# Hybrid decoder layer on one core: four raw weight tiles, the up products in another order, the gate as one function

## The chip, the cores and the metric

One Trainium2 chip, one core. The metric is the device time of one execution in microseconds (us); the kernel before takes 2186.93 us, the median of 3 runs (2183.86 to 2192.37).

## The reference

A decoder layer over 1024 positions of width 1024, in fp32: a gated feed-forward part (FFN) with half weight, a token-mixing part (RWKV-7 beside a chunked gMLP, from one input projection into one output projection), a second FFN, and a last norm.

```python
def swiglu(h, w1, w3, w2):
    return (jax.nn.silu(h @ w1) * (h @ w3)) @ w2

for l in range(DEPTH):            # DEPTH = 1, D_MODEL = 1024, D_FF = 2816
    x = x + FFN_RES_SCALE * swiglu(rmsnorm(x, ffn1_norm[l]), ffn1_w1[l], ffn1_w3[l], ffn1_w2[l])
    h = rmsnorm(x, mix_norm[l])
    p = h @ w_in[l]
    y_rwkv = rwkv7_mixer(p[..., :D_SHIFT], ...)
    y_gmlp = gmlp_mixer(p[..., D_SHIFT:D_SHIFT + GMLP_WIDTH], p[..., D_SHIFT + GMLP_WIDTH:], ...)
    x = x + jnp.concatenate([y_rwkv, y_gmlp], axis=-1) @ w_out[l]
    x = x + FFN_RES_SCALE * swiglu(rmsnorm(x, ffn2_norm[l]), ffn2_w1[l], ffn2_w3[l], ffn2_w2[l])
return rmsnorm(x, final_norm)
```

## The kernel before

**Numbers and products.** Every large fp32 product is made of three fp32r matmuls: each operand is held as a high part (ACT copies it into the fp32r tile) and a low part (DVE or POOL subtract the high part from the source), and the three of the four pairs in `HI_LO` are accumulated in PSUM. The positions are two halves ("rows") of 512, the features likewise. Each FFN matrix product is done with seven products of half-sized operands instead of eight, by sums and differences of the quarters; the products are numbered 1 to 7.

**Stages of an FFN.**
- `first_half` does product 1 of both up matrices with row 0: 22 steps (w1 and w3 by turns, 11 column blocks), 24 matmuls each. Its result goes to DRAM (`sd`) for the other products; its gated value goes to `hd[1]`.
- Meanwhile a background task, `build`, makes the operands of products 3 to 7 (`x_build`: per round of four, four tiles `nx` are loaded, all four normed on DVE (L297), added and subtracted, and split into `xc`). When it is done, its pool is closed, a new pool `pw` is opened and the first weights `wraw` are loaded into it.
- `up` does products 6, 5, 7, 4, 3 in 22 steps of 60 matmuls (L192 issues all of them, `prod` takes 12 per product). `up_prep` makes the five weight operands of the step ahead on DVE (L386 to L392) and splits them into `wup`, a ring of eight. Five PSUM evacuations on DVE (L447, L451, L453, L458, L462) add the products to `s1`; product 7 is accumulated in the bank of product 6 and product 3 in that of product 5. On even steps (w1) the gate is a tanh on ACT (L327) and one DVE operation (L328), on odd steps (w3) a DVE product (L330). Every second step `out` makes `hd[2]` to `hd[7]` on POOL and stores them.
- `down` does products 1, 5, 2, 3, 6, 7, 4, each in 11 steps of 12 matmuls. A step's `operands` loads a weight tile and a tile of `hd` into one `raw` tile (ring of two; L479, L480 issue the loads on SP's queue), combines the weight with `tst` on DVE (L483 in product 5, L485 in 7, L487 in 4, L495 in 3), copies both halves on ACT (L490, L491) and subtracts on DVE (L492, weight) and POOL (L493, h) into a `wsp` tile (ring of four). After a product DVE adds its banks to the residual tiles `rd` or `res` (L527); a finished residual is squared (L230 on ACT, L232 on DVE).

A norm's sum of squares goes over the partitions by `spread`: 8 small matmuls, a power on POOL (L220), and 4 matmuls that spread it back (L201).

**The mixer** stands between the FFNs: `w_in`, `lora_up`, gMLP, the RWKV chain as background work, `w_out`. Its weight tiles come through the same ring `raw` of two (`wtile`, `w_out`). `lora_up` makes three results per block in an `xs` tile (ring of two) and a `silu` tile (ring of three), and stores each to DRAM (L875). `first_half` of FFN2 starts with row 0; at its step 12 at the latest a hook puts in `w_out` of row 1, then the remaining steps follow, with `build` beside them.

**What sets the order.** The program is written as generators. `Flow` steps them by a clock of its own (the numbers behind `yield`), the tile framework then orders each engine's instructions by priority (`evac()` puts the evacuations of PSUM ahead) and by its own timing of them, and each engine works through its list in that order. Weight loads and most stores share SP's queue. A tile of a ring comes free, and its next load may be issued, only when its last reader is done.

## Time and profile before

| | |
|---|---|
| median of 3 runs | 2186.93 us (2183.86 to 2192.37) |
| profiled execution, its own time | 2188.83 us |
| its span in the trace | 2187.0 us |
| mean granted clock of TensorE | 0.956 |
| busy: PE, weight loads | 1999.5 us (91%), 1617.7 us (74%) |
| busy: DVE, ACT, POOL | 1272.0 us (58%), 702.2 us (32%), 987.7 us (45%) |
| HBM read, written | 260.53 MB, 93.34 MB |
| stages: first_half of FFN1, its up, its down | 25.9 to 160.5, to 472.4, to 738.2 us |
| mixer with w_out and FFN2's first_half, up's start | to 1593.65 us |
| up of FFN2, its down, last spread and output | to 1903.8, to 2166.0, to 2187.0 us |

PE is TensorE's matmuls, PEld its weight loads. Busy time counts an instruction from its start to its end; idle time before an instruction is put down to what released it last. The granted clock is the share of TensorE's full speed that the throttle gave; matmul durations in the records overlap, so the price of one is best taken from a run of many.

### The profile page before, as it was taken

Reading aid. Unit: us, or ns where it says so; the run is one execution under the profiler, and the core shown is the slowest. Engines: PE = TensorE matmul, PEld = TensorE weight load, DVE = VectorE, ACT = ScalarE, POOL = GpSimd, SP = SyncE. Lnnn points to the kernel's source line nnn. Section 1 sums busy time; section 2 is a strip of 40 time slices with the busy share of each in tenths; the row PEclk is TensorE's granted clock in tenths of the full one; section 3 lists DMA queues with packets and bytes.
Section 4 is the critical chain, followed back from the end, with each engine's and each line's share of the span. In section 5 each row is a group of like instructions: output and inputs, shape, how many; then the busy total and the mean of one; then the engine's idle time right before and its main releaser. Section 6 shows DMA issues by size and latency. Waiting matters only on the chain.

```text
span 2187.0 us, 34516 instructions
## 1 busy us (share of the span) xinstructions
PE 1999.5 (91%) x13408; PEld 1617.7 (74%) x13408; DVE 1272.0 (58%) x1749; ACT 702.2 (32%) x1202; POOL 987.7 (45%) x749
## 2 busy tenths in 40 slices
PE   6999999997998998999999989989789999979986
PEld 5777777786776677777888778867577777858764
DVE  7828777745457464454543354324877777544565
ACT  5442222213444443252212232224422222224432
POOL 4426666643444664353322232223566666434432
PEclk9999999998998999998999997999989999989988
DMA  6754444435544577453534463336644444375443
GB/s 217 239 170 160 151 160 164 165 141 209 187 135 150 180 258 218 114 202 106 172 101 118 121 191 109 119 112 211 223 148 148 148 158 164 110 251 181 133 153 116
DMA packets 232884, 356.15 MB, mean 163 GB/s; under 512 B 67984, under 2 KB 100752, under 8 KB 232720
## 3 DMA queue, kind: packets, MB, share of 16 engines
q1 hardware_dynamic: 178944, 338.23, 46.5%
q10 hardware_dynamic: 53776, 15.71, 3.1%
q8 instruction: 105, 1.72, 0.3%
q14 instruction: 59, 0.48, 0.1%
HBM read 260.53 MB, written 93.34 MB: 162 GB/s over the span
## 4 chain that ended last, share of the span: by engine, by line
PE 22%; DMA 11%; DVE 8%; issue 5%; POOL 3%; ACT 1%; SPq 0%; POOLq 0%; ACTq 0%; DVEq 0%
PE psd L192 12%; PE pse L192 4%; PE pse L201 3%; DMA raw<-in_ffn_w_dram 3%; DMA raw<-hd 2%; PE psc L201 2%; DMA wraw<-in_ffn_w_dram 1%; POOL wsp L493 1%; DMA raw<-in_w_out_dram 1%; POOL wsp L712 1%; DVE wsp L492 1%; DVE rd L527 1%; POOL wup L257 1%; DMA tdr<-D 1%; DMA M<-ldr 1%
## 5 line engine op out<-in xcount | busy, mean ns | idle before, releaser
L192 PE MATMUL psd<-xt,wsp 128*128 128x512 f32 x1920 | 484.7, 408 | 19.4 <-ACT silu L353 9.0
L192 PEld LDWEIGHTS psd<-xt,wsp 128*128 128x128 f32 x1920 | 363.6, 193 | 115.7 <-ACT silu L353 12.1
L192 PE MATMUL psd<-xc,wup 128*128 128x512 f32 x1584 | 376.0, 394 | 37.2 <-DVE z L447 20.3
L192 PEld LDWEIGHTS psd<-xc,wup 128*128 128x128 f32 x1584 | 298.0, 189 | 108.7 <-DVE z L447 23.8
L712 POOL TENSOR_TENSOR wsp<-raw,wsp 128x512 fp32r<-128x512 f32 x170 | 234.3, 1398 | 317.7 <-ACT wsp L709 317.5
L192 PE MATMUL psd<-wsp 128*128 128x512 f32 x1440 | 351.0, 402 | 27.4 <-ACT wsp L491 14.9
L192 PEld LDWEIGHTS psd<-wsp 128*128 128x128 f32 x1440 | 274.0, 193 | 97.5 <-ACT wsp L491 16.7
L493 POOL TENSOR_TENSOR wsp<-raw,wsp 128x512 fp32r<-128x512 f32 x154 | 210.3, 1368 | 293.7 <-ACT wsp L491 241.3
L257 POOL TENSOR_TENSOR wup<-wraw,wup 128x512 fp32r<-128x512 f32 x132 | 200.6, 1528 | 117.7 <-ACT wup L256 112.4
L192 PE MATMUL pse<-xc,wup 128*128 128x512 f32 x1056 | 248.0, 390 | 0.0
L192 PEld LDWEIGHTS pse<-xc,wup 128*128 128x128 f32 x1056 | 198.4, 188 | 41.4 <-ACT wup L256 0.2
L709 ACT CAST wsp<-raw 128x512 fp32r<-128x512 f32 x246 | 140.5, 618 | 152.5 <-PE psd L192 58.2
L492 DVE TENSOR_TENSOR wsp<-raw,wsp 128x512 fp32r<-128x512 f32 x110 | 96.2, 876 | 104.8 <-ACT wsp L490 104.3
L256 ACT CAST wup<-wraw 128x512 fp32r<-128x512 f32 x132 | 81.1, 619 | 223.5 <-PE pse L192 151.8
L192 PE MATMUL pse<-wsp 128*128 128x512 f32 x396 | 118.3, 416 | 31.2 <-DVE wsp L492 18.1
L491 ACT CAST wsp<-raw 128x512 fp32r<-128x512 f32 x154 | 95.4, 620 | 124.2 <-DMA raw<-hd 114.2
L490 ACT CAST wsp<-raw 128x512 fp32r<-128x512 f32 x110 | 68.0, 618 | 195.2 <-DMA raw<-in_ffn_w_dram 107.8
L192 PEld LDWEIGHTS pse<-wsp 128*128 128x128 f32 x396 | 75.2, 197 | 59.3 <-DVE wsp L492 22.0
L192 PE MATMUL psc<-wsp 128*128 128x512 f32 x396 | 111.6, 408 | 0.0
L257 POOL TENSOR_TENSOR wup<-wt,wup 128x512 fp32r<-128x512 f32 x44 | 63.4, 1440 | 69.7 <-ACT wup L256 58.7
L256 ACT CAST wup<-wt 128x512 fp32r<-128x512 f32 x88 | 53.6, 617 | 120.3 <-PE psd L192 100.9
L192 PEld LDWEIGHTS psc<-wsp 128*128 128x128 f32 x396 | 78.4, 199 | 17.5
(216 smaller groups left out, 2620.6 us busy)
## 6 DMA issues: line engine op xcount, KB each, us to landing
wraw<-in_ffn_w_dram SPq DMA_DIRECT2D x88, 512.0 KB, 4.5
raw<-hd SPq DMA_DIRECT2D x154, 256.0 KB, 3.3
raw<-in_ffn_w_dram SPq DMA_DIRECT2D x132, 256.0 KB, 3.1
raw<-in_ffn_w_dram SPq DMA_DIRECT2D x44, 512.0 KB, 4.0
raw<-in_w_in_dram SPq DMA_DIRECT2D x36, 512.0 KB, 3.6
hd<-u SPq DMA_DIRECT2D x66, 256.0 KB, 2.0
hd<-s SPq DMA_DIRECT2D x66, 256.0 KB, 2.1
sd<-silu SPq DMA_DIRECT2D x44, 256.0 KB, 3.2
```

Source lines behind the costliest of these rows:

```text
L192: i = self.nc.tensor.matmul(*args, **kw)
L201: i = self.nc.tensor.matmul(*args, **kw)
L256: nc.scalar.copy(t[:, 0], src)
L257: eng.tensor_tensor(t[:, 1], src, t[:, 0].bitcast(F32), op=ALU.subtract)
L490: nc.scalar.copy(t[:, 0, 0], w)
L491: nc.scalar.copy(t[:, 0, 1], h)
L492: ve.tensor_tensor(t[:, 1, 0], w, t[:, 0, 0].bitcast(F32), op=ALU.subtract)
L493: ge.tensor_tensor(t[:, 1, 1], h, t[:, 0, 1].bitcast(F32), op=ALU.subtract)
L527: ve.scalar_tensor_tensor(rv, sets[y][f], 0.25, rv, op0=ALU.mult, op1=ALU.add)
L709: self.nc.scalar.copy(dst[:, 0, sl], src[:, sl])
L712: eng.tensor_tensor(dst[:, 1, sl], src[:, sl], dst[:, 0, sl].bitcast(F32), op=ALU.subtract)
```

## The change

It has five parts.
- The ring `raw` has four tiles (`RAWB`) instead of two, in `wtile`, `down` and `w_out`; `wsp` keeps four. To make room, squares are put elsewhere (in row 1 of FFN1's down into a `raw` tile), `lora_up` puts its three results into three `silu` tiles, and in `up` the ring `z` has 3 tiles for 6, `s` 4 for 5, with `s1` in a ring of its own of 3.
- `up` does products 6, then 4 of the step before, 5, 7, 3. Products 6 and 7 have banks of their own (`d`), as 5 and 3 have (`e`); product 4 is accumulated on its step's product 7. There are still five evacuations per step. `up_prep` splits product 3's weight ahead of product 4's.
- The gate on even steps is ACT's Silu alone; the factor in `down` goes from 0.25 to 0.5, since the tanh form gave twice the value.
- `apply` stores row 0's normed tiles to DRAM (`xn`), and `x_build` loads them instead of norming row 0 again.
- In FFN2, `pw` is opened and the first weights are loaded ahead of `x_build`, and row 1's spread stands right behind `w_out`.

```diff
+RAWB = 4
...
-    def squares(self, pool, acc, t):
+    def squares(self, pool, acc, t, name="xs", bufs=2):
...
-            s = pool.tile([P, 2, HALF], F32, name="xs", bufs=2)
+            s = pool.tile([P, 2, HALF], F32, name=name, bufs=bufs)
...
-    def apply(self, dst, res, gain, rb):
+    def apply(self, dst, res, gain, rb, out=None):
...
+            if out is not None:
+                nc.sync.dma_start(out[k], t)
...
-            nc.sync.dma_start(t, src[row][k // 2][:, k % 2])
+            nc.sync.dma_start(t, src[row][k // 2][:, k % 2] if row else self.xn[k])
...
-            for k, t in zip(ks, ts):
-                normed(*k, t)
+            for k, t in zip(ks[:2], ts):
+                ve.scalar_tensor_tensor(t, t, self.v(gain, k[1]), rb[0], op0=ALU.mult, op1=ALU.mult)
...
-                nc.scalar.activation(u, c, AF.Tanh, scale=0.5)
-                nc.vector.scalar_tensor_tensor(u, u, 1.0, c, op0=ALU.add, op1=ALU.mult)
+                nc.scalar.activation(u, c, AF.Silu)
...
+        ws[3] = sp(b22, ge)
         ws[4] = sp(b21, ge)
-        ws[3] = sp(b22, ge)
...
-        def z(name="z", bufs=6):
+        def z(name="z", bufs=3):
...
-                s1s[s] = z()
+                s1s[s] = z("s1", 3)
...
-            b, c = self.psum("d"), self.psum("e")
-            s1 = s1s.pop(s)
-            yield from prod(s, 6, b, True, False)
-            with self.evac():
-                w12 = z()
-                ve.tensor_add(w12, b, s1)
-            yield from prod(s, 5, c, True, False)
-            yield from prod(s, 7, b, False, True)
-            with self.evac():
-                ve.tensor_add(s1, b, s1)
-                w22 = z()
-                ve.tensor_add(w22, c, s1)
-            self.gate(us, u, s, 22, w22)
-            d = self.psum("d")
-            yield from prod(s, 4, d, True, True)
-            with self.evac():
-                ve.tensor_add(s1, d, s1)
-            self.gate(us, u, s, 21, s1)
-            yield from prod(s, 3, c, False, True)
-            with self.evac():
-                ve.tensor_add(w12, c, w12)
-            self.gate(us, u, s, 12, w12)
+        def tail(s, b, w12):
+            yield from prod(s, 4, b, False, True)
+            with self.evac():
+                ve.tensor_add(w12, b, w12)
+            self.gate(us, u, s, 21, w12)
...
+            s1 = s1s.pop(s)
+            a = self.psum("d")
+            yield from prod(s, 6, a, True, True)
+            with self.evac():
+                w12 = s1
+                ve.tensor_add(w12, a, s1)
+            if last is not None:
+                yield from tail(*last)
+            c = self.psum("e")
+            yield from prod(s, 5, c, True, True)
+            with self.evac():
+                v = z()
+                ve.tensor_add(v, c, w12)
+            b = self.psum("d")
+            yield from prod(s, 7, b, True, False)
+            with self.evac():
+                w22 = z()
+                ve.tensor_add(w22, b, v)
+            self.gate(us, u, s, 22, w22)
+            d = self.psum("e")
+            yield from prod(s, 3, d, True, True)
+            with self.evac():
+                ve.tensor_add(v, d, v)
+            self.gate(us, u, s, 12, v)
+            last = (s, b, w12)
+        yield from tail(*last)
...
-            raw = self.ws.tile([P, 2, HALF], F32, name="raw", bufs=2)
+            raw = self.ws.tile([P, 2, HALF], F32, name="raw", bufs=RAWB)
...
-                        ve.scalar_tensor_tensor(rv, sets[y][f], 0.25, rv, op0=ALU.mult, op1=ALU.add)
+                        ve.scalar_tensor_tensor(rv, sets[y][f], 0.5, rv, op0=ALU.mult, op1=ALU.add)
...
-    def build(self, src, gain, w, rb, stats, ready):
+    def build(self, src, gain, w, rb, stats, ready, early=False):
...
+        if early:
+            self.pw, self.cpw = self.open("pw")
         pool, cb = self.open("pb")
         yield from stats(pool)
+        if early:
+            self.raw0 = self.up_load(self.pw, w, 0)
         yield from self.x_build(pool, self.xc, src, gain, rb)
...
-                self.squares(self.xq, accs[row], res[row][kp])
+                self.squares(*((self.ws, accs[1], res[1][kp], "raw", RAWB) if row else (pool, accs[0], res[0][kp])))
...
-            yield from self.w_out(1, xres, accs[1])
+            p1, c1 = self.open("p1")
+            yield from self.w_out(1, xres, accs[1], (p1,))
 
             def stats2(pool):
-                cxq.close()
-                rb = yield from self.spread(accs[1], "e")
-                rbs2.append(self.keep(rb, pool))
-
-            flow.spawn(self.build(xres[1], "g2", w2, rbs2, stats2, ("xb", 1)))
+                yield 0.1
+                rbs2.append(self.keep(rb1, pool))
+
+            rb1 = yield from self.spread(accs[1], "e")
+            c1.close()
+            cxq.close()
+            flow.spawn(self.build(xres[1], "g2", w2, rbs2, stats2, ("xb", 1), True))
...
-                    t = self.xq.tile([P, 2, HALF], F32, name="xs", bufs=2)
-                    ts = [t[:, 0], t[:, 1], self.xtp.tile([P, HALF], F32, name="silu", bufs=3)]
+                    ts = [self.xtp.tile([P, HALF], F32, name="silu", bufs=3) for _ in range(3)]
```

Three places in the order of the instructions. On PE, from w_out of row 1 (`psd<-wsp`) over the rest of first_half (`psd<-xt,wsp`) to the first up product (`psd<-xc,wup`), `one,xs` and `con,rr_r` being the spread, before:

```order
L192 MATMUL psd<-wsp 128x512 x192
L192 MATMUL psd<-xt,wsp 128x512 x33
L201 MATMUL pse<-one,xs 128x1 x8
L192 MATMUL psd<-xt,wsp 128x512 x9
L201 MATMUL pse<-con,rr_r 128x128 x4
L192 MATMUL psd<-xt,wsp 128x512 x174
L192 MATMUL psd<-xc,wup 128x512 x2
```

and now:

```order
L193 MATMUL psd<-wsp 128x512 x192
L202 MATMUL pse<-one,xs 128x1 x8
L202 MATMUL pse<-con,rr_r 128x128 x4
L193 MATMUL psd<-xt,wsp 128x512 x216
L193 MATMUL psd<-xc,wup 128x512 x2
```

The spread's two groups stood among the matmuls of first_half and now stand ahead of them.

On DVE, at the end of product 1 of FFN2's down (`wsp<-raw` are its last splits, `dt` the weights kept for the later products, combined for product 5, and `rd<-psd` the evacuations of product 1), before:

```order
L492 TENSOR_TENSOR wsp<-raw,wsp 128x512 x7
L483 TENSOR_TENSOR dt<-raw,dt 128x512
L492 TENSOR_TENSOR wsp<-dt,wsp 128x512
L527 SCALAR_TENSOR_TENSOR rd<-psd,rd 128x512 x3
L483 TENSOR_TENSOR dt<-raw,dt 128x512
L527 SCALAR_TENSOR_TENSOR rd<-psd,rd 128x512 x9
L483 TENSOR_TENSOR dt<-raw,dt 128x512
L492 TENSOR_TENSOR wsp<-dt,wsp 128x512
L483 TENSOR_TENSOR dt<-raw,dt 128x512
```

and now:

```order
L502 TENSOR_TENSOR wsp<-raw,wsp 128x512 x7
L493 TENSOR_TENSOR dt<-raw,dt 128x512 x2
L502 TENSOR_TENSOR wsp<-dt,wsp 128x512
L493 TENSOR_TENSOR dt<-raw,dt 128x512
L502 TENSOR_TENSOR wsp<-dt,wsp 128x512
L493 TENSOR_TENSOR dt<-raw,dt 128x512
L537 SCALAR_TENSOR_TENSOR rd<-psd,rd 128x512 x3
L502 TENSOR_TENSOR wsp<-dt,wsp 128x512
L537 SCALAR_TENSOR_TENSOR rd<-psd,rd 128x512 x9
L493 TENSOR_TENSOR dt<-raw,dt 128x512
```

Three more combinations and one more split of product 5 now stand ahead of the first evacuations.

On SP, at the start of FFN2's down (`dt` the kept weights, `raw` the operands' loads, `hd_10` stores of the last up step), before:

```order
L677 DMA rd<-xres_1_3_98 128x1024
L514 DMA dt<-in_ffn_w_dram 128x512 x6
L479 DMA raw<-in_ffn_w_dram 128x512
L480 DMA raw<-hd_6_153 128x512
L514 DMA dt<-in_ffn_w_dram 128x512
L479 DMA raw<-in_ffn_w_dram 128x512
L480 DMA raw<-hd_7_154 128x512
L514 DMA dt<-in_ffn_w_dram 128x512 x4
```

and now:

```order
L428 DMA hd_10_201<-s 128x512
L696 DMA rd<-xres_1_3_98 128x1024
L430 DMA hd_10_223<-u 128x512
L524 DMA dt<-in_ffn_w_dram 128x512 x2
L432 DMA hd_10_212<-s 128x512
L524 DMA dt<-in_ffn_w_dram 128x512 x2
L435 DMA hd_10_179<-s 128x512
L524 DMA dt<-in_ffn_w_dram 128x512 x4
L489 DMA raw<-in_ffn_w_dram 128x512
L490 DMA raw<-hd_8_155 128x512
```

The stores of the last step now stand among the loads, and where six loads of `dt` stood ahead of the load for step 6 (`hd_6`), eight stand ahead of that for step 8.

## Rows read from the trace of the kernel before

**Rows 1.** Page, part 1: busy us, share of span and instructions of each engine.

```profile
PE 1999.5 (91%) x13408; PEld 1617.7 (74%) x13408; DVE 1272.0 (58%) x1749; ACT 702.2 (32%) x1202; POOL 987.7 (45%) x749
```

**Rows 2.** Chain that ended last, in up of FFN2: start us, us, engine, tile, line, count.

```profile
1871.32 8.16 PE psd L192 x36
```

**Rows 3.** Stretches, L192: window, length, PE busy, PEld busy, granted clock, DMA share, GB/s.

```profile
160.50:474.90 314.40, 302.58 (x1320) 246.70 (x1321) 1.00 0.44 150
...
472.40:738.20 265.80, 233.06 (x937) 180.54 (x936) 0.94 0.54 179
...
1511.30:1593.60 82.30, 57.38 (x220) 43.20 (x220) 0.88 0.66 221
...
1593.60:1911.90 318.30, 309.31 (x1340) 253.25 (x1341) 0.99 0.41 144
...
1903.80:2165.90 262.10, 228.88 (x937) 178.92 (x935) 0.95 0.53 173
...
2048.90:2078.80 29.90, 29.90 (x134) 24.75 (x133) 1.00 0.44 127
...
2078.80:2127.60 48.80, 36.09 (x133) 26.32 (x132) 0.86 0.43 145
```

**Rows 4.** Timeline of PE, start of FFN2's second half: start us, us, instruction [idle before].

```profile
1511.33 9.49 PE L192 MATMUL psd<-xt,wsp 128*128 128x512 f32 x33 [4.80 <-DVE res L760]
...
1584.52 1.22 PE L192 MATMUL psd<-xc,wup 128*128 128x512 f32 x2 [7.60 <-ACT wup L256]
...
1593.65 4.65 PE L192 MATMUL psd<-xc,wup 128*128 128x512 f32 x12 [7.05 <-DVE wup L257]
```

**Rows 5.** Timeline of PE, down of both FFNs.

```profile
506.42 10.95 PE L192 MATMUL psd<-wsp 128*128 128x512 f32 x36 [4.94 <-ACT wsp L491]
...
2092.15 1.65 PE L192 MATMUL pse<-wsp 128*128 128x512 f32 x3 [4.54 <-DVE wsp L492]
```

**Rows 6.** Waits of ACT in down: us in total, times, longest us.

```profile
ACT wsp L491 <- DMA raw<-hd: 114.2, 71, 8.0
...
ACT wsp L490 <- DMA raw<-in_ffn_w_dram: 107.8, 43, 15.9
```

**Rows 7.** Page, part 6, DMA issues: loads of raw, KB each, median us to landing.

```profile
raw<-in_ffn_w_dram SPq DMA_DIRECT2D x132, 256.0 KB, 3.1
```

**Rows 8.** Groups of DVE in down: busy us, mean ns, idle us before and its releasers.

```profile
L492 DVE TENSOR_TENSOR wsp<-raw,wsp 128x512 fp32r<-128x512 f32 x110 | 96.2, 876 | 104.8 <-ACT wsp L490 104.3
...
L232 DVE TENSOR_TENSOR xs<-xs 128x1024 f32<-128x1024 f32 x24 | 32.4, 1350 | 23.6 <-ACT xs L230 23.6
...
L527 DVE SCALAR_TENSOR_TENSOR rd<-psd,rd 128x512 f32<-128x512 f32 x44 | 28.0, 678 | 0.9 <-PE psd L192 0.9
...
L485 DVE TENSOR_TENSOR raw<-dt,raw 128x512 f32<-128x512 f32 x22 | 19.3, 877 | 28.0 <-DMA raw<-in_ffn_w_dram 26.1 <-DMA raw<-hd 1.9
```

**Rows 9.** Waits of PE: for the evacuation of product 6 of up.

```profile
PE psd L192 <- DVE z L447: 20.3, 12, 2.6
```

**Rows 10.** Timeline of PE, last spread of the program.

```profile
2170.75 3.57 PE L201 MATMUL pse<-one,xs 128*128 128x1 f32 x16 [4.71 <-DVE xs L232]
...
2175.66 2.08 PE L201 MATMUL pse<-con,rr_r 128*128 128x128 f32 x8 [1.34 <-POOL rr_r L220]
```

**Rows 11.** Group of DVE in x_build: the normalisation.

```profile
L297 DVE SCALAR_TENSOR_TENSOR nx<-nx,vec,rbk 128x512 f32<-128x512 f32 x32 | 33.1, 1050 | 7.2 <-ACT rbk L280 3.6 <-DMA nx<-xres 3.2 <-DMA nx<-in_x_dram 0.4
```

**Rows 12.** Line L875, lora_up's stores: ns min/median/max on SP, us to landing.

```profile
L875 SPq DMA_DIRECT2D lo<-xs x16: 319/452/1362, 775.4 to 972.4; - x16
...
DMA to landing us min/median/max: 2.0/3.5/6.4
```

**Rows 13.** Groups of the gate and of ACT's table loads.

```profile
L328 DVE SCALAR_TENSOR_TENSOR u<-u,z 128x512 f32<-128x512 f32 x66 | 61.6, 937 | 23.9 <-ACT u L327 23.9
...
L1043 ACT ACT_TABLE_LOAD x2 | 2.6, 1283 | 2.3 <-DVE gmean L1235 2.3
```

**Rows 14.** Line L390, DVE in the preparation of up's weights: ns min/median/max.

```profile
L390 DVE TENSOR_TENSOR wraw<-wraw x44: 677/1750/1784, 90.4 to 1871.0; 128x512 f32<-128x512 f32 x44
```

More of the change, by code (lines that the diff above doesn't have):

```diff
@@ L292, in load @@
             t = new()
-            nc.sync.dma_start(t, src[row][k // 2][:, k % 2])
+            nc.sync.dma_start(t, src[row][k // 2][:, k % 2] if row else self.xn[k])
             return t
-        def normed(row, k, t):
-            ve.scalar_tensor_tensor(t, t, self.v(gain, k), rb[row], op0=ALU.mult, op1=ALU.mult)
         def put(p, kk, t, eng):
@@ L466, in up @@
             ws.pop(s)
+        u = lambda: z("u", 6)
+        prep(0)
+        last = None
+        for s in range(ns):
+            prep(s + 1)
+            s1 = s1s.pop(s)
[24 more added lines that the diff above has]
+        yield from tail(*last)
     def down(self, pool, w2, res, done):
@@ L534, in build @@
                    for p in (6, 5, 7, 4, 3)}
+        if early:
+            self.pw, self.cpw = self.open("pw")
         pool, cb = self.open("pb")
         yield from stats(pool)
+        if early:
+            self.raw0 = self.up_load(self.pw, w, 0)
         yield from self.x_build(pool, self.xc, src, gain, rb)
         cb.close()
-        self.pw, self.cpw = self.open("pw")
-        self.raw0 = self.up_load(self.pw, w, 0)
+        if not early:
+            self.pw, self.cpw = self.open("pw")
+            self.raw0 = self.up_load(self.pw, w, 0)
         self.flow.done.add(ready)
@@ L571, in program @@
         self.hd = {p: [self.dr.tile([P, HALF], F32, name=f"hd{p}_{j}") for j in range(NP)] for p in range(1, 8)}
+        self.xn = [self.dr.tile([P, HALF], F32, name=f"xn{k}") for k in range(KT)]
         self.sd = [self.dr.tile([P, HALF], F32, name=f"sd{j}") for j in range(2 * NP)]
@@ L580, in program @@
         x12 = self.halves()
-        rbs = [self.keep(rb)]
-        self.apply(x12, rx, "g1", rb)
+        rbs = []
+        self.apply(x12, rx, "g1", rb, self.xn)
         cb.close()
@@ L644, in program @@
         accs = ([], [])
-        out0 = yield from self.w_out(0, xres, accs[0])
+        out0 = yield from self.w_out(0, xres, accs[0], (self.mp, "h", 3))
         rb = yield from self.spread(accs[0], "e")
-        rbs2 = [self.keep(rb)]
+        rbs2 = []
         x12 = self.halves()
-        self.apply(x12, out0, "g2", rb)
+        self.apply(x12, out0, "g2", rb, self.xn)
         state = {"done": False}
@@ L714, in wtile @@
     def wtile(self, shape, src, eng=None):
-        raw = self.ws.tile([P] + list(shape), F32, name="raw", bufs=2)
+        raw = self.ws.tile([P] + list(shape), F32, name="raw", bufs=RAWB)
         self.nc.sync.dma_start(raw, src)
@@ L733, in dense_T, with w_out @@
         return o
-    def w_out(self, half, xres, acc):
+    def w_out(self, half, xres, acc, sums):
         nc = self.nc
@@ L745, in w_out @@
             for n, k in enumerate([4, 5, 6, 7, 0, 1, 2, 3]):
-                raw = self.ws.tile([P, 2, HALF], F32, name="raw", bufs=2)
+                raw = self.ws.tile([P, 2, HALF], F32, name="raw", bufs=RAWB)
                 nc.sync.dma_start(raw[:, 0], wv[k, :, hc])
@@ L760, in w_out @@
                         nc.vector.tensor_add(r[:, i], r[:, i], ps[2 * j + i])
-                self.squares(self.xq, acc, r)
+                self.squares(*sums[:1], acc, r, *sums[1:])
                 nc.sync.dma_start(xres[1][half][hf * 2 + j], r)
```

10 lines of the change are left out of this document (3 added, 7 removed).

## The prediction

> **What bounds the kernel now.** I read the busy shares first: TensorE (PE) is busy for 1999.5 of 2187.0 us, 91%, VectorE (DVE) for 58%, POOL for 45%, ScalarE (ACT) for 32% [rows 1]. The median of the runs is 2186.93 us; the profiled execution took 2188.83, so 1.8 us lie around its span and it is 1.9 above the median. So the floor is PE's matmuls, and what can be won is the time in which PE waits. The chain of waits gives their price: 36 matmuls of 128x512 in 8.16 us, 0.2267 us each [rows 2]. I then hold each stage against its number of matmuls by that price, with the table by stretch [rows 3]:
> - the five up products of FFN1: 314.4 us for 1320 matmuls (299.2), of FFN2: 318.3 for 1340 (303.8). Excess 15.2 and 14.5, together 30.
> - down of FFN1: 265.8 us for 937 (212.4), of FFN2: 262.1 for 937 (212.4). Excess 53.4 and 49.7, together 103. It isn't spread evenly: product 6 of FFN2 stands at the floor (29.90 us), product 7 behind it takes 48.80, and the granted clock has a mean of 0.86 there, so part of it ran at 1.2 instead of 2.4 GHz.
> - from w_out's end to the up products of FFN2: 82.3 us, and 4.80 of idle before them [rows 3, 4], 87.1 in all, for 220 matmuls (49.9).
>
> So the excess in these stages is some 170 us. The timeline of PE says what ends these waits: in down the copies and splits of the weight tile, 4.94 us behind ACT's copy of h and 4.54 behind DVE's subtraction [rows 5]. Who is late there? ACT waited 107.8 us for the weights in `raw` and 114.2 for `raw`'s h half [rows 6], with 3.1 us from issue to landing [rows 7]. A step of down has 12 matmuls, 2.72 us; a ring of two `raw` tiles, each held for landing, copies and both subtractions, can't turn round in two steps (3.1, then 0.88 of DVE's subtraction [rows 8], ACT's two copies and POOL's subtraction, before any wait in a queue). The loads are issued late because their tile comes free late.
>
> **The change part by part.**
> *Four raw tiles (A).* It removes no instruction; each load may be issued two steps, 5.4 us, earlier. Bounds: 0 to 103 us. What is late next is DVE: product 7 has 11 L485 at 0.877, 11 L492 at 0.876, and into it fall the 12 evacuations of product 6 at 0.678 and two additions of squares at 1.350 [rows 8]: 19.3 + 8.1 + 2.7 = 30.1 us against PE's 29.9. That fits only just, and the evacuations come in one piece of 8 us with priority over the subtractions. On the other hand three more combinations and one more split of the next product now stand ahead of that piece at the end of product 1. I take three fifths, 62.
>
> *Order of the up products (B).* Today product 7 goes on in product 6's bank, and can't start before DVE's L447 has read it; only product 5 lies between. PE waited 20.3 us for L447 [rows 9]. In the new order product 6 has a bank to itself and the tail of the step before and product 5 lie between it and the next use of such a bank. The number of matmuls and of PSUM evacuations per step stays. Bounds 0 to 30; I take 20, the row's own sum.
>
> *Start of FFN2's up (C).* The row says what stands there: PE waits 7.60 and 7.05 us for the first `wup` tiles, since the weights are loaded only once the build's pool is closed [rows 4]. With the weights loaded early and the spread ahead of first_half's rest, what is left is the spread alone, with no matmuls beside it; the end of the kernel shows one such: 4.71 + 3.57 + 1.34 + 2.08 = 11.7 us [rows 10]. Then 216 matmuls (49.0), some 2 us of start and, as the clock drops around idle time (today 0.88 is granted in the stage, and PE is busy for 57.38 us with matmuls worth 49.9 [rows 3]), 6 for matmuls below full clock: 69. That is 18 less than 87.1. x_build is covered: without row 0's normalisation (16 of the 32 L297 at 1.050 [rows 11] go) DVE has about 36 us there, an estimate of nine operations in each of four rounds at that row's price, beside 49 of matmuls. Were that cover gone, 36 would stand bare and C be lost. Bounds 8 (all four small waits come back) to 25.
>
> *Normed half through DRAM (D).* 16 stores more on SP in two places, 0.452 us of issue each at the median [rows 12]: 7.2 us in which SP's next weight loads stand behind them. Bounds 0 to -7; -2, since first_half's ring is now twice as deep.
>
> *lora_up on three `silu` tiles (E).* A block's three results take all three tiles of that ring, so the next block's evacuation waits until the stores land: median 3.5 us [rows 12]. Two halves with three such waits: 21 us at most; PSUM lets two blocks of products run ahead. Bounds 0 to -21; -8.
>
> *Gate as one function (G).* 66 + 22 DVE operations go (L328, 61.6 us in the 66 [rows 13]). On DVE in up they aren't on the path: PE waits for L447 alone there, whose own cost is counted in B. ACT loads its tables seven times where it did four; the two existing loads of one line took 1.283 each [rows 13], 3.9 us for three, on an engine that is 32% busy, at the starts of stages: 0, and 3.9 if its cover is gone. The Trainium skill ("ScalarE: Activation LUTs", What ACT_TABLE_LOAD costs) has a drain of about 1.38 us with each switch and so speaks against a change that mixes sets: by it the three are some 8 us, an estimate, and the sum 2103 if all of it lay on the path.
>
> *Deeper ring in w_out and w_in (F).* The same tiles there; most gaps of the mixer have other causes. 0 to 10; 2.
>
> Sum: 62 + 20 + 18 - 2 - 8 + 2 = 92 us, span 2095.0, execution 2096.8, and as the profiled one stood 1.9 above the median, **2095 us**.
>
> **The rivals.**
> 1. *All waits go.* A 103, B 30, C 21, the costs as above: 146 to 150, some 2037 to 2055 us. For it: product 6 at its floor with the same ring [rows 3]. Against it: DVE's 30.1 for 29.9 in product 7.
> 2. *Down is bound by DVE, not by the loads.* L390, a DVE operation with both inputs in SBUF, shows 0.677 at best and 1.750 at the median [rows 14], with POOL at work beside it. If earlier loads only put POOL's h subtractions on top of DVE's, L485 and L492 go to 1.75: 38.5 + 8.1 + 2.7 = 49.3 for product 7, what it takes now. Then the products that combine weights (5, 7 and 4) keep their time and only the others gain, put at a fifth of the 103: A 20, 2137 us. The Trainium skill ("SBUF — State Buffer", Who interferes with whom) has a rule of this kind, an exclusive lock of a port pair shared by DVE and GpSimd; the trace agrees so far as L390's two prices go. Against it: today's means of 0.877 and 0.876 are with POOL at work too.
> 3. *The deeper ring isn't used*: SP takes its rows in order, and the loads stand behind stores that wait for other engines. A 0, B 10, C 8, costs of 8: gain 10, 2177 us. For it: SP's order mixes stores of `hd` and loads at the start of down. Against it: it does so at the start only.
> 4. *Slower: weights of up come late.* Product 4's pair of `wup` tiles is now held over product 6 of the next step, out of a ring of eight where a step takes five. If the splits of a step so start one product later and the slack doesn't cover it, each of 44 steps waits for 12 matmuls, 2.72 us: +119.7, B lost, 2187.0 + 119.7 - 72 = 2235. It decides where the wait for a split exceeds the one product of slack. Against it: the two existing waits for `wup` lie at the start alone [rows 4], and the stages keep 95% of floor speed.
>
> **How the numbers follow.** Forecast 0.55; rival 1 0.15, rival 2 0.18, rival 3 0.06, rival 4 0.06. The range of 2045 to 2150 takes in the forecast with A between 30 and 100, rival 2, and the upper part of rival 1; rivals 3 and 4 and the lowest of rival 1 stay out, under 0.2. The ends of all bounds together would be 2019 and 2207. A measurement here tells 0.5%, 10.9 us, from no change: faster 0.90 (forecast, rivals 1 and 2, a third of 3), same 0.04 (the rest of 3), slower 0.06 (rival 4).
>
> **What would show it.** Right: both downs at 225 to 245 us, their products 30 to 36 each, ACT's waits for `raw` far below 100 us; no wait of PE for the evacuation of product 6, the up stages near 300 us; about 12 us of bare spread behind w_out and a start of up without waits over 3 us; seven table loads, none ahead of a wait of PE. Wrong: product 7 still at 45 with DVE busy all through it (rival 2); ACT still waiting 100 us for `raw` (3); PE waiting for `wup` in every step (4); or new gaps in lora_up over 10 us in each half (E mis-sized).

## The result, and the profile after

The changed kernel takes 2120.47 us (median of 4 runs, 2119.34 to 2122.47) against 2185.39 for the kernel before: a ratio of 0.9704, 95% interval 0.9671 to 0.9738. The forecast was 2095, the range 2045 to 2150. The profiled execution after has a span of 2117.5 us, 69.5 below the one before.

The page's busy shares after; the columns are those of [rows 1]:

```profile
PE 1976.5 (93%) x13408; PEld 1615.9 (76%) x13408; DVE 1156.0 (55%) x1645; ACT 697.9 (33%) x1203; POOL 976.4 (46%) x749
```

PE has the same 13408 matmuls. DVE has lost 104 instructions (66 + 22 of the gate, 16 of x_build) and 116 us; whether PE waited for any of them is asked below. The stretches of the table by window after, for L193 (L192 before), columns as in [rows 3]; in order up of FFN1, its down, product 7 of that, the mixer up to w_out, w_out of row 1, from there to up, up of FFN2, its down, products 7 and 4 of that:

```profile
161.50:465.30 303.80, 303.73 (x1332) 250.91 (x1333) 0.99 0.47 158
460.00:708.30 248.30, 222.81 (x937) 178.87 (x936) 0.95 0.57 192
619.10:672.10 53.00, 34.90 (x134) 25.66 (x132) 0.86 0.36 119
708.30:1209.40 501.10, 299.94 (x1305) 225.20 (x1304) 0.94 0.51 154
...
1445.00:1493.80 48.80, 46.43 (x192) 37.25 (x192) 0.96 0.69 237
1493.80:1565.20 71.40, 55.10 (x217) 42.85 (x216) 0.88 0.59 193
1565.20:1868.70 303.50, 303.46 (x1332) 251.12 (x1333) 0.99 0.47 158
1863.50:2097.50 234.00, 219.66 (x937) 177.68 (x935) 0.98 0.57 189
...
2024.40:2067.60 43.20, 34.44 (x134) 26.65 (x133) 0.92 0.55 180
2067.60:2097.50 29.90, 29.90 (x133) 24.55 (x131) 1.00 0.33 104
```

The same stretches before, cut at the first and last matmul of each stage in the same way (up of FFN1, product 7 of its down, mixer, w_out of row 1, from there to up, up of FFN2; the downs are in [rows 3]):

```profile
160.50:478.30 317.80, 305.98 (x1335) 249.51 (x1336) 1.00 0.44 150
652.80:698.10 45.30, 34.65 (x133) 25.46 (x132) 0.89 0.40 129
738.20:1226.80 488.60, 293.65 (x1306) 220.59 (x1305) 0.95 0.52 159
...
1460.80:1506.40 45.60, 45.58 (x192) 36.90 (x192) 0.96 0.55 174
1506.40:1584.50 78.10, 55.43 (x217) 42.04 (x216) 0.93 0.66 220
1584.50:1909.70 325.20, 309.18 (x1335) 252.56 (x1336) 0.98 0.41 145
```

| stretch | before | after | |
|---|---|---|---|
| up of FFN1 | 317.8 | 303.8 | -14.0 |
| down of FFN1 | 265.8 | 248.3 | -17.5 |
| mixer up to w_out | 488.6 | 501.1 | +12.5 |
| w_out of row 1 | 45.6 | 48.8 | +3.2 |
| from there to up | 78.1 | 71.4 | -6.7 |
| up of FFN2, its first waits among it | 325.2 | 303.5 | -21.7 |
| down of FFN2 | 262.1 | 234.0 | -28.1 |

So the FFNs gave 88 us, the mixer and w_out of row 1 took 16 back, and the stretches that aren't listed 3. Where the gain of the downs came from, ACT's waits say (us in total, times, longest; [rows 6] before):

```profile
ACT wsp L500 <- DMA raw<-in_ffn_w_dram: 17.0, 5, 9.5
...
ACT wsp L501 <- DMA raw<-hd: 15.3, 6, 6.5
```

222 us of ACT's waiting for `raw` have become 32. DVE's own waits for `raw` in product 7 have not gone: L485 before waited 28.0 us for these loads [rows 8], the same line after (L495) 15.3 + 11.9 = 27.2 (busy us, mean ns, idle before and its releasers):

```profile
L495 DVE TENSOR_TENSOR raw<-dt,raw 128x512 f32<-128x512 f32 x22 | 15.3, 696 | 31.1 <-DMA raw<-in_ffn_w_dram 15.3 <-DMA raw<-hd 11.9 <-POOL wsp L503 3.0
```

Nor did every product of the downs gain. Products 2, 3 and 6 stand at the floor of 29.9 us in both. Product 7 of FFN2 went from 48.8 to 43.2, but that of FFN1 from 45.3 to 53.0.

No wait of PE for product 6's evacuation is left ([rows 9] had 20.3 us), and both up stages run at PE's price: 1332 matmuls by 0.2267 are 302. Where time was lost shows best at the end of FFN1's down, in the timeline of PE after (start, length, instruction, idle before); its first line is the start of product 4:

```profile
672.10 28.05 PE L193 MATMUL psd<-wsp 128*128 128x512 f32 x110 [7.91 <-ACT wsp L501]
...
706.31 2.11 PE L193 MATMUL psd<-wsp 128*128 128x512 f32 x8
708.36 1.09 PE L819 MATMUL pse<-wT,ones 128*64 128x128 f32 x14
713.99 3.58 PE L202 MATMUL pse<-one,raw 128*128 128x1 f32 x16 [4.55 <-DVE raw L233]
717.43 2.91 PE L193 MATMUL psd<-xt,wsp 128*128 128x512 f32 x6
```

The spread of row 1 (`one,raw`) now stands ahead of the mixer's first matmuls, and 9 us go by without a matmul of 128x512. The 7.91 us ahead of product 4 are inside the 53.0 us of product 7. DVE's timeline shows what comes ahead of product 4's first combination (L497) there: eight evacuations of product 7 and the sum of a square that ACT has just made.

```profile
663.54 2.48 DVE L537 SCALAR_TENSOR_TENSOR res<-pse,res 128x512 f32<-128x512 f32 x4
665.93 2.47 DVE L537 SCALAR_TENSOR_TENSOR res<-psc,res 128x512 f32<-128x512 f32 x4
668.99 1.23 DVE L233 TENSOR_TENSOR raw<-raw 128x1024 f32<-128x1024 f32 x1 [0.58 <-ACT raw L231]
670.13 0.68 DVE L497 TENSOR_TENSOR raw<-raw,dt 128x512 f32<-128x512 f32 x1
```

With two raw tiles (`e1_raw2` below) the first step of product 4 comes without a wait.

### The profile page after: what moved, and what is told of

The parts are those of the page before. It is cut to its first block, busy times and chain, and to the rows that moved or that the text cites. A ratio compares the mean times of both kernels' runs of the same rounds, so it can differ in the third digit from the quotient of the medians.

```text
span 2117.5 us, 34486 instructions
## 1 busy us (share of the span) xinstructions
PE 1976.5 (93%) x13408; PEld 1615.9 (76%) x13408; DVE 1156.0 (55%) x1645; ACT 697.9 (33%) x1203; POOL 976.4 (46%) x749
## 3 DMA queue, kind: packets, MB, share of 16 engines
q1 hardware_dynamic: 181248, 342.43, 48.8%
## 5 line engine op out<-in xcount | busy, mean ns | idle before, releaser
L193 PE MATMUL psd<-xt,wsp 128*128 128x512 f32 x1920 | 490.9, 413 | 11.8 <-DVE wsp L731 5.8
L193 PEld LDWEIGHTS psd<-xt,wsp 128*128 128x128 f32 x1920 | 370.1, 196 | 107.7 <-DVE wsp L731 7.1
L731 POOL TENSOR_TENSOR wsp<-raw,wsp 128x512 fp32r<-128x512 f32 x170 | 231.0, 1378 | 361.5 <-ACT wsp L728 344.4
L193 PE MATMUL psd<-xc,wup 128*128 128x512 f32 x1584 | 377.3, 391 | 3.6 <-ACT wup L257 3.6
L193 PE MATMUL psd<-wsp 128*128 128x512 f32 x1440 | 341.4, 396 | 14.6 <-ACT wsp L501 9.6
L193 PEld LDWEIGHTS psd<-xc,wup 128*128 128x128 f32 x1584 | 299.0, 189 | 67.3 <-ACT wup L257 4.5
L193 PEld LDWEIGHTS psd<-wsp 128*128 128x128 f32 x1440 | 272.5, 191 | 75.7 <-ACT wsp L501 10.5
L503 POOL TENSOR_TENSOR wsp<-raw,wsp 128x512 fp32r<-128x512 f32 x154 | 229.4, 1495 | 214.4 <-ACT wsp L501 170.2
L193 PE MATMUL pse<-xc,wup 128*128 128x512 f32 x1056 | 255.0, 390 | 0.0
L258 POOL TENSOR_TENSOR wup<-wraw,wup 128x512 fp32r<-128x512 f32 x132 | 178.6, 1360 | 124.7 <-ACT wup L257 121.4
L193 PEld LDWEIGHTS pse<-xc,wup 128*128 128x128 f32 x1056 | 198.5, 188 | 41.4 <-ACT wup L257 0.2
L502 DVE TENSOR_TENSOR wsp<-raw,wsp 128x512 fp32r<-128x512 f32 x110 | 104.6, 961 | 78.7 <-ACT wsp L500 78.5
L385 DVE TENSOR_TENSOR wt<-wraw 128x512 f32<-128x512 f32 x44 | 43.2, 981 | 180.8 <-DMA wraw<-in_ffn_w_dram 180.8
L193 PE MATMUL pse<-wsp 128*128 128x512 f32 x396 | 112.8, 413 | 14.7 <-DVE wsp L502 10.0
L193 PE MATMUL psc<-wsp 128*128 128x512 f32 x396 | 105.5, 396 | 1.9 <-DVE wsp L502 1.9
L731 DVE TENSOR_TENSOR wsp<-raw,wsp 128x512 fp32r<-128x512 f32 x76 | 61.7, 847 | 81.9 <-ACT wsp L728 75.8
L193 PEld LDWEIGHTS pse<-wsp 128*128 128x128 f32 x396 | 77.5, 199 | 36.8 <-DVE wsp L502 15.3
L501 ACT CAST wsp<-raw 128x512 fp32r<-128x512 f32 x154 | 94.7, 616 | 20.8 <-DMA raw<-hd 15.3
L193 PEld LDWEIGHTS psc<-wsp 128*128 128x128 f32 x396 | 75.4, 191 | 18.8 <-DVE wsp L502 2.8
```

The source lines that it names most:

```text
L193: i = self.nc.tensor.matmul(*args, **kw)
L258: eng.tensor_tensor(t[:, 1], src, t[:, 0].bitcast(F32), op=ALU.subtract)
L385: ve.tensor_sub(t1, b12, b11)
L501: nc.scalar.copy(t[:, 0, 1], h)
L502: ve.tensor_tensor(t[:, 1, 0], w, t[:, 0, 0].bitcast(F32), op=ALU.subtract)
L503: ge.tensor_tensor(t[:, 1, 1], h, t[:, 0, 1].bitcast(F32), op=ALU.subtract)
```

## The experiments

Each starts from the changed kernel; where it builds on another run, the text says so. `...` marks what is left out of an edit.

**Two raw tiles again** (`e1_raw2`):

```diff
-RAWB = 4
+RAWB = 2
...
-                self.squares(*((self.ws, accs[1], res[1][kp], "raw", RAWB) if row else (pool, accs[0], res[0][kp])))
+                self.squares(*((self.xq, accs[1], res[1][kp]) if row else (pool, accs[0], res[0][kp])))
```

> The changed kernel with two raw tiles instead of four; the squares of row 1 go to an xs ring of two as before. Theory (the ring of four is what sped up both downs, and squares in raw tiles are what laid the spread of row 1 bare at the end of FFN1's down): both downs go back to 262 and 266 us, +46; the start of the mixer gets its 9 us back and product 7 of FFN1's down 5 to 8 us; in all 2120 + 46 - 9 = 2157 us, 2145 to 2165. Rival (the downs gained from the gate or other relief of DVE): no change in the downs, 2105 to 2120 us.

Measured: 2170.42 us median, ratio to the kernel before 0.9924 (0.9886 to 0.9963). Its two downs, by window:

```profile
456.50:720.70 264.20, 230.76 (x937) 178.15 (x936) 0.95 0.54 180
1883.40:2146.20 262.80, 228.65 (x937) 178.01 (x935) 0.95 0.52 172
```

Both downs are back at their old lengths, and so are ACT's waits for `raw` (96.7 and 127.7 us). The ring of four is worth 527.0 - 482.3 = 44.7 us there. The edit moves the squares too, but they matter little for that: `e6_one_sq_tile` keeps four tiles, moves the squares, and its downs take 484.9 us. The total missed the range by 5 us. The mixer did start without the bare spread, but its whole came out no shorter (503.0 us). And two tiles cost time where the expectation had none: w_out of row 1 took 52.8 us and the way from there to up 76.5 (52.6 and 76.6 in the next run), where the changed kernel has 48.8 and 71.4.

**lora_up on its old tiles, with two raw tiles** (`e2_raw2_lora`, built on `e1_raw2`):

```diff
-                    ts = [self.xtp.tile([P, HALF], F32, name="silu", bufs=3) for _ in range(3)]
+                    t = self.xq.tile([P, 2, HALF], F32, name="xs", bufs=2)
+                    ts = [t[:, 0], t[:, 1], self.xtp.tile([P, HALF], F32, name="silu", bufs=3)]
```

> As the run with two raw tiles, and lora_up's results in an xs tile and a silu tile as before. Theory (three silu tiles make each block wait for its stores): 6 to 12 us less than the run with two raw tiles alone. Rival (PSUM lets the products run ahead, the stores are hidden): within 3 us of it.

Measured: 2164.54 us, 5.9 below the run before, just outside the range; the spans of the two profiled executions are the same, 2166.7 us. The stretches with lora_up in them (from the end of down on, and in the second half), first with three `silu` tiles (`e1_raw2`), then with the old tiles:

```profile
720.70:804.20 83.50, 71.62 (x269) 51.35 (x269) 0.96 0.67 221
943.80:978.00 34.20, 23.57 (x77) 15.26 (x77) 0.90 0.66 225
```

```profile
723.50:800.30 76.80, 68.29 (x270) 49.24 (x269) 1.00 0.69 236
942.80:970.30 27.50, 21.69 (x78) 13.89 (x77) 1.00 0.70 246
```

6.7 us in each half, 13.4 together: the three tiles do make lora_up wait for its stores (in the changed kernel DVE and ACT wait 17.8 and 3.6 us for `lo<-silu` in its two lines; with the old tiles no such wait is left). More than half of it is given back before w_out (503.0 against 497.5 us up to there).

**The old order of the up products** (`e3_old_up`; the rings `z` 6 and `s` 4 with it):

```diff
-            a = self.psum("d")
-            yield from prod(s, 6, a, True, True)
+            b, c = self.psum("d"), self.psum("e")
+            yield from prod(s, 6, b, True, False)
...
-            if last is not None:
-                yield from tail(*last)
...
+            yield from prod(s, 5, c, True, False)
+            yield from prod(s, 7, b, False, True)
...
```

> The changed kernel with the old order of the up products (6, 5, 7, 4, 3, banks shared by 6 and 7 and by 5 and 3); gate and all else as changed. Theory (the order took away the wait for product 6's evacuation): PE waits 20 us for it again, each up stage 7 to 14 us longer, 2135 to 2148 us. Rival (the gate's relief of DVE did it): up stages as changed, 2120 us within 4.

Measured: 2145.05 us. PE's waits and the two up stages:

```profile
PE psd L193 <- DVE z L446: 18.3, 9, 2.7
```

```profile
161.40:478.80 317.40, 309.04 (x1335) 252.90 (x1336) 0.98 0.43 150
1577.10:1897.00 319.90, 309.55 (x1335) 253.17 (x1336) 0.98 0.42 149
```

The wait for product 6's evacuation (L446 here) is back with 18.3 us, and the stages are 13.6 and 16.4 us longer, 30.0 together: the whole gain of up hangs on the order, its banks and rings with it, with the new gate in both.

**The old order and the old gate** (`e4_old_up_tanh`, built on `e3_old_up`):

```diff
-                nc.scalar.activation(u, c, AF.Silu)
+                nc.scalar.activation(u, c, AF.Tanh, scale=0.5)
+                nc.vector.scalar_tensor_tensor(u, u, 1.0, c, op0=ALU.add, op1=ALU.mult)
...
```

> The old order of the up products and the gate as tanh and DVE operation, all else as changed. Theory (the gate is off the path): within 4 us of the run with the old order alone. Rival (DVE's 88 operations delay the evacuations): 8 to 15 us more than that run.

Measured: 2150.97 us, 5.9 more than the run before, between the two expectations. Its up stages are 317.7 and 317.9 us long, against 317.4 and 319.9: with the old order, the gate gives nothing there; with the new one it wasn't tested. The 5.9 us of the medians (2.5 in the spans) lie in other stages and are less than what the last paragraph of this section shows of the mixer alone.

**lora_up in a raw tile** (`e5_lora_raw`):

```diff
-                    ts = [self.xtp.tile([P, HALF], F32, name="silu", bufs=3) for _ in range(3)]
+                    t = self.ws.tile([P, 2, HALF], F32, name="raw", bufs=RAWB)
+                    ts = [t[:, 0], t[:, 1], self.xtp.tile([P, HALF], F32, name="silu", bufs=3)]
```

> The changed kernel, but lora_up takes a raw tile (ring of four) for two of its three results and one silu tile for the third. Theory (each block waits for the stores of the three silu tiles, some 4 to 7 us per half): 2120 - 11 = 2109 us, with both lora stretches 4 to 7 us shorter. Rival (what lora loses is given back where the mixer waits for its chain anyway): the stretches are shorter, the whole within 4 us of 2120.

Measured: 2113.83 us (2105.37 to 2116.12), 6.6 below the change, but not for the reason given. Its stretches with lora_up got longer, 94.5 and 47.5 us, where the changed kernel has 89.1 and 34.3:

```profile
706.60:801.10 94.50, 72.12 (x269) 53.09 (x269) 0.89 0.59 201
935.20:982.70 47.50, 21.59 (x77) 13.82 (x76) 0.86 0.67 228
```

A result waiting for its store in `raw` keeps a tile from the weights; that this is the cause is argued from the ring, not tested. The expectation failed. The mixer up to w_out took 503.8 us, against 501.1, so the stretches between those with lora_up are shorter; why stays open, and the total lies within what the last paragraph of this section shows of the mixer alone.

**One raw tile for the squares of row 1** (`e6_one_sq_tile`):

```diff
+    def squares1(self, acc, t):
...
+            if not acc:
+                r = self.ws.tile([P, 2, HALF], F32, name="raw", bufs=RAWB)
+                acc += [r[:, 0:1], r[:, 1]]
+                nc.scalar.activation(r[:, 0], t[:, 0], AF.Square, scale=1.0 / 32)
...
+            for k in ks:
+                nc.scalar.activation(acc[1], t[:, k], AF.Square, scale=1.0 / 32)
+                nc.vector.tensor_add(acc[0][:, 0], acc[0][:, 0], acc[1])
...
```

> The changed kernel, but the squares of row 1 in FFN1's down take one raw tile in all (sum in one half, the new square in the other) instead of one for the sum and one for each new square. Theory (the squares hold the tiles that the loads of the mixer's first weights need, so the spread lies bare for 9 us): first matmul of the mixer 7 to 9 us earlier behind down, 2111 to 2114 us if it isn't given back later. Rival (ACT's order puts the squares ahead in any case): still 9 us bare, 2120 us.

Measured: 2108.93 us, ratio to before 0.9658 (0.9619 to 0.9698), 11.5 us below the change and the fastest complete version of the study; the interval of its ratio still overlaps that of the change (0.9671 to 0.9738). The timeline of PE behind down:

```profile
709.33 1.09 PE L838 MATMUL pse<-wT,ones 128*64 128x128 f32 x14
710.35 10.77 PE L193 MATMUL psd<-xt,wsp 128*128 128x512 f32 x45
720.96 0.95 PE L202 MATMUL pse<-one,raw 128*128 128x1 f32 x8
```

The mixer's matmuls follow at once, 8 us earlier behind down, and cover the spread; down of FFN1 itself took 251.8 us, 3.5 more than in the changed kernel. So the squares' tiles laid the spread bare. By which way is argued: in the changed kernel the sum of squares and each new square took a raw tile apiece, and the mixer's first weights were loaded at 703.16, 5 us ahead of down's end, where here the load is issued at 691.55, 18 us ahead. But ACT's order differs as well: there its copies of these weights stand behind the squares, here the first ones ahead of them. The run doesn't part the two.

**No early load** (`e7_no_early`): `build` is called without `True`, so the weights are loaded behind x_build again.

> The changed kernel without the early load: pw is opened and the first up weights are loaded behind x_build, as before; the spread stays where the change put it. Theory (the early load took away the two waits for wup at the start of up, 7.6 and 7.1 us, and costs w_out 3 us of DVE): from w_out's end to the steady up 10 to 15 us longer, w_out of row 1 3 us shorter, 2127 to 2132 us. Rival (x_build ends early enough since it norms half as much): within 4 us of 2120.

Measured: 2116.02 us. w_out of row 1, from there to up, and up:

```profile
1452.30:1496.70 44.40, 44.39 (x192) 36.50 (x192) 0.98 0.65 220
1496.70:1567.60 70.90, 53.63 (x217) 41.84 (x216) 0.93 0.66 218
1567.60:1870.80 303.20, 302.50 (x1331) 249.69 (x1332) 1.00 0.47 158
```

The rival was right: without the early load the start of up is as short (70.9), and w_out is 4.4 us shorter: in the changed kernel DVE prepares up's first weights (L385 to L391) between w_out's splits, at 1459.0 to 1469.4.

**No normed half in DRAM** (`e8_no_xn`): x_build loads row 0 from `src` and norms all four tiles, `apply` stores nothing.

> The changed kernel without the normed half in DRAM: x_build loads row 0 from its source and norms it again (16 operations of DVE more), apply stores nothing. Theory (D costs a few us at FFN1's start and saves DVE time that the matmuls of first_half cover): first_half of FFN1 2 to 4 us shorter, 2114 to 2122 us. Rival (x_build was late for up): the start of up of FFN2 8 to 17 us later, 2128 to 2137 us.

Measured: 2113.38 us. FFN1's first_half is 2.5 us shorter, but its start 3.4 later; from w_out to the end of up it is 74.3 + 303.9 = 378.2 us against 374.9. Neither the early load nor the half in DRAM is worth much by itself.

**Product 7 without its combination** (`e9_p7_no_combination`):

```diff
-            elif p == 7:
-                ve.tensor_sub(w, tst[jj], w)
```

> The changed kernel without the combination of the weight in product 7 (11 DVE operations per down, L497; the raw weight is used in its place, so product 7's values are not the reference's). Theory (what is left of product 7's excess is DVE's work): product 7 of FFN2's down from 43 to 31 to 36 us, of FFN1's down from 53 to 41 to 46, 2100 to 2108 us. Rival (the loads or ACT's copies are late): product 7 within 2 us of 43 and 53, 2120 us.

Product 7's combination is L495 in the changed kernel; L497, which the expectation names, is product 4's. Measured: 2108.43 us. Product 7 of both downs, first the changed kernel, then this one, with the busy time of every engine (PE, PEld, DVE, ACT, POOL), then the granted clock:

```profile
2024.40:2067.60 43.20, 36.90 (x158) 29.40 (x157) 30.33 (x44) 14.50 (x24) 16.19 (x13) 0.92 0.55 180
619.10:672.10 53.00, 38.98 (x158) 30.00 (x156) 38.38 (x52) 18.96 (x31) 18.88 (x14) 0.86 0.36 119
```

```profile
2020.00:2056.40 36.40, 35.47 (x158) 28.31 (x158) 25.70 (x35) 13.34 (x22) 15.28 (x12) 0.95 0.61 197
619.00:664.80 45.80, 36.78 (x157) 29.68 (x155) 35.03 (x45) 18.71 (x31) 19.49 (x14) 0.88 0.39 132
```

Taking 11 DVE operations from each product 7 shortens it by 6.8 and 7.2 us. That is more than the scatter: in the other runs with four tiles product 7 took 42.2 to 46.7 us in FFN2 and 49.1 to 53.0 in FFN1. So the rival's outcome failed, and the combination is worth half of FFN2's excess of 13.3 us and a third of FFN1's 23.1. It doesn't show that DVE is short of time: DVE was idle for 12.9 of the 43.2 us, 8.5 of them ahead of this very line, waiting for the loads. The edit takes a link out of the chain of load, combination, copy and split as well as work from DVE, and the run can't tell these apart. What is left stays in part open; in FFN1 7.02 us of it are the wait ahead of product 4, which is still there. In FFN1 DVE has 8 us more in the stretch, the normed operand of the mixer's row 0.

**The spread of row 1 back among first_half** (`e10_spread_back`, with one tile for squares and no early load):

```diff
...
-            p1, c1 = self.open("p1")
-            yield from self.w_out(1, xres, accs[1], (p1,))
+            yield from self.w_out(1, xres, accs[1], ())
...
-                yield 0.1
+                cxq.close()
+                rb1 = yield from self.spread(accs[1], "e")
                 rbs2.append(self.keep(rb1, pool))
...
-            rb1 = yield from self.spread(accs[1], "e")
-            c1.close()
-            cxq.close()
-            flow.spawn(self.build(xres[1], "g2", w2, rbs2, stats2, ("xb", 1), True))
+            flow.spawn(self.build(xres[1], "g2", w2, rbs2, stats2, ("xb", 1)))
...
```

> The changed kernel with one tile for the squares of row 1 (in FFN1's down and in w_out of row 1), no early load, and the spread of row 1 back among the matmuls of first_half, as before the change. Theory (the start of FFN2's up gained from the spread's place, since x_build starts when it is done): from w_out's end to the end of up 8 to 14 us longer than in the run without the early load (71 + 303), 2115 to 2125 us. Rival (it gained from x_build's half as many normalisations): spread covered, so 8 to 12 us shorter or the same, 2098 to 2108 us.

Measured: 2118.26 us. From w_out to the end of up 65.8 + 314.7 = 380.5 us, 6.4 more than without the early load alone (374.1), less than the 8 to 14 expected. In the timeline the two waits for `wup` are back:

```profile
1550.35 1.22 PE L193 MATMUL psd<-xc,wup 128*128 128x512 f32 x2 [4.59 <-ACT wup L273]
...
1561.55 3.78 PE L193 MATMUL psd<-xc,wup 128*128 128x512 f32 x8 [9.13 <-DVE wup L274]
```

So it was the spread's place that took away the 7.60 and 7.05 us of [rows 4], and the bare spread costs about half of that again. The edit also puts w_out's squares into a raw tile; but the next run, with the spread in its new place and neither early load nor half in DRAM, has waits of 2.31 and 0.80 us there, so the place is what counts.

**Three of these together** (`e11_best`: one tile for squares, no early load, no half in DRAM), and the same **with POOL for four of DVE's subtractions** (`e12_best_pool`):

> The changed kernel with one tile for the squares of row 1 in FFN1's down, without the early load and without the normed half in DRAM, which cost or gave nothing each by itself. Theory (they add up): 2120 - 11 - 4 - 5 = 2100 us, 2094 to 2106. Rival (without both, x_build and the first weights come late together): start of up later by 8 us or more, 2108 to 2115 us.

> As the run before, and POOL does all eight subtractions of the mixer's row 0 operand that fall into product 7 of FFN1's down, four of which DVE did. Theory (DVE binds product 7): product 7 of FFN1's down 3 to 6 us shorter than there, 4 us less in all. Rival (POOL is as late): no change within 3 us.

Measured: 2121.90 and 2119.93 us. They don't add up. From w_out to the end of up it is 381.2 us without both, against 374.1 and 378.2 without one: each of the two covered for the other, at least in part. The rest is the mixer, 504.0 us up to w_out where `e6_one_sq_tile` has 491.1 with the same code there. POOL's share made product 7 of FFN1's down 49.8 us instead of 51.2, which is within its scatter, so the rival held: no change within 3 us.

How far can the mixer be read at all? `e6_one_sq_tile` and `e10_spread_back` have the same order of the 128x512 matmuls on PE from the mixer's start to w_out of row 1, and the part up to the first w_out took 491.1 and 495.1 us; the change and `e7_no_early` too have one order, and took 501.1 and 509.7. Between most other pairs many rows on PE stand differently, since the scheduler moves background work about for any edit. Totals of these runs that differ by less than some 10 us are therefore not put down to an edit here; the up stages are (FFN1's repeats within 1.5 us in the runs with the new order), and the products of the downs where a difference exceeds their scatter. So the mixer's 12.5 us in the table above, too, are a sum of which only the parts seen in timelines are put down to causes.

## Why the prediction was right, and where its terms were off

The direction, the bound (PE's waits in down and up) and the range held; the forecast was 25 us too low. That it was no further off is in part luck: A, C and the costs were 31 us too hopeful, and B's 10 us in the other direction made up for some of it. Two of its signs of being right failed: FFN1's down took 248.3 us, not 225 to 245, and products 5 and 7 took 36.0 to 53.0, not 30 to 36. By its steps, in us gained:

| step | forecast | measured | from |
|---|---|---|---|
| A, four raw tiles | 62 | 45 | downs of `e1_raw2` against the change |
| B, order of up | 20 | 30 | up stages of `e3_old_up` |
| C, start of FFN2's up | 18 | 12 | 403.3 - 374.9 from w_out to the end of up, less B's 16.4 in that stage |
| D, E, F: stores, lora_up, mixer | -8 | -16 | mixer and w_out of row 1, table above; the squares' 9 and the early load's 4 are in it |
| G, gate | 0 | 0 in up | `e4_old_up_tanh`, old order |

*A was mis-sized.* It took three fifths of the excess; 45 of 103 came. The loads were the reason for what came, as put: ACT's waits for `raw` fell from 222 to 32 us, products 2, 3 and 6 stand at the floor, and product 1 of FFN1 lost 12.2 us. What did not come is mostly product 7: of the 57 us of excess left in the downs it has 13.3 and 23.1. The prediction costed DVE's work there as fitting only just, 30.1 for 29.9 us. That sum left work out: the same trace has eight more operations in product 7 of FFN2, 5.4 us for the output (L687; L706 after), and in FFN1 5.6 + 3.1 us for the mixer's operand (L274, L262). And this work comes in pieces. The timeline of DVE in product 7 of FFN2 after shows nine of the twelve evacuations in 6.1 us, and later the output's eight in one piece:

```profile
2025.69 1.88 DVE L537 SCALAR_TENSOR_TENSOR rd<-psd,rd 128x512 f32<-128x512 f32 x3
2027.48 0.68 DVE L495 TENSOR_TENSOR raw<-dt,raw 128x512 f32<-128x512 f32 x1
2028.08 3.67 DVE L537 SCALAR_TENSOR_TENSOR rd<-psd,rd 128x512 f32<-128x512 f32 x6
...
2047.40 5.35 DVE L706 SCALAR_TENSOR_TENSOR rd<-rd,vec,psd 128x512 f32<-128x512 f32 x8
```

PE's longest wait in this product, 2.64 us for a split, ends behind the second piece. Sums over a product hide this: DVE was busy for 30.3 of 43.2 us. The prediction's second rival was right in part about which products would stay: product 5 took 36.0 us in FFN1 and 38.9 in FFN2 before, 36.6 and 36.0 after; product 7 is told above; and only product 4 of FFN2 lost its excess (38.3 to 29.9). Its mechanism isn't what held product 7 of FFN2, though: the price of its combination did not go to 1.75 beside POOL but fell from 0.877 to 0.696 in the mean (L495, at most 0.836), and the split's there is 0.711 (1.011 in FFN1). Both prices stand elsewhere, as in product 4's combination, 0.674 and 1.781 (ns min, median, max):

```profile
L497 DVE TENSOR_TENSOR raw<-raw,dt x22: 674/786/1781, 670.1 to 2086.8; 128x512 f32<-128x512 f32 x22
```

The rule of the Trainium skill ("SBUF — State Buffer", Who interferes with whom) that DVE with two SBUF inputs contends with GpSimd's reads would explain the upper one. The trace after agrees: all 11 of these above 0.76 us start while an instruction runs on POOL, and 2 of the 11 short ones; of the evacuations (L537), which have one input in PSUM, 33 of 96 start so, and none takes over 0.692 us. No run here takes POOL away.

*B was right in mechanism and too small.* The row of waits (20.3) counts PE's idle time alone; the stage's whole excess of 30 hung on the order. The other 10 don't stand as idle time in the records but as matmuls that took longer: with the old order (`e3_old_up`) PE was busy for 309.0 and 309.6 us with 1335 matmuls worth 302.6, at a mean granted clock of 0.98, and in the new one for 303.7 and 303.5 with 1332 worth 302.0, at 0.99.

*C: the mechanism was named wrongly in part.* "The weights are loaded only once the build's pool is closed" was taken for the cause of the two waits for `wup`. `e7_no_early` undoes just that and loses nothing while row 0 comes normed from DRAM; `e10_spread_back` moves the spread back and the waits return. x_build waits for the spread, and the spread stood behind 42 matmuls. The early load was costed at nothing on the path, and takes 4.4 us in w_out. (Nine operations in each of four rounds at 1.050 are 37.8 us, not 36; nothing hung on it.)

*E and the squares.* lora_up's wait was found and sized 8; with two raw tiles it is 13.4 locally, and more than half of it is given back. What no term had is the other cost of the ring: row 1's squares were said to be "put elsewhere" and costed at nothing. They are put into the ring that the mixer's first weights need, and lay the spread bare for 9 us; `e6_one_sq_tile` gets 8 of them back, and loses 3.5 in down. *F*, the deeper ring elsewhere, was sized 2 and is more: `e1_raw2` takes 4.0 us longer in w_out of row 1 and 5.1 from there to up, and these 5.1 stand in C's 12.

*G.* Seven table loads of 1.283 us instead of four, on an engine that is 33% busy, cost nothing that shows in up. The first of the gate starts 0.80 us after the work before it, and the next operation follows at once (timeline of ACT):

```profile
45.73 1.28 ACT L327 ACT_TABLE_LOAD   x1 [0.80 <-issue]
47.03 0.60 ACT L327 ACTIVATE silu<-psd 128x512 f32<-128x512 f32 x1
```

By the Trainium skill ("ScalarE: Activation LUTs", What ACT_TABLE_LOAD costs) a drain of some 1.38 us comes with each switch. The trace doesn't show one of that length as idle time of ACT: four of the seven loads (at 762.0, 838.6, 952.0 and 1124.9 us) start 0.02 us behind the work before them, and after this one and most others the next operation starts 0.01 us behind the load. Rivals 3 and 4 fell: the loads do come earlier, and PE's waits for `wup` in the whole program are 3.6 us.

## What to carry to other kernels

A ring's depth is bought from other tiles: ask of each tile that moves what it now shares a ring with, and who loads into that ring next. Before an excess over the floor is put down as won, list everything the next engine does in that stretch, and look at the pieces in which it comes, not at its sum alone. And where two waits stand behind one event, undo the candidates one at a time: here the load that seemed late wasn't what PE waited for.

## What had not been expected of the hardware

Two pairs of runs with the same order of large matmuls on PE differ by 4.0 and 8.6 us in the mixer, while the up stages of the same kernels stay between 302.4 and 303.8 us where the spread is as changed. PE ran 1332 matmuls of up at 0.228 us each, 303.73 us busy of 303.80, with a granted clock of 0.99; in the stretches with waits the mean of the granted clock was lower, 0.86 in product 7 with 53.0 us, so that the waits went along with slower matmuls and cost more than their own length: there 134 records of matmuls were busy for 34.90 us, where product 6 of FFN2, without waits, took 29.90 at 1.00 [rows 3].
